# A hybrid decoder trunk on one core: the pre-norm applied in the transposition by a diagonal matrix, the first tiles in a fixed order, keys and values post-processed for all tiles at once

## The chip, the cores and the metric

The kernel runs on one core of a Trainium2 chip. The core has five engines with queues of their own: TensorE (PE in the profile, its weight loads PEld), VectorE (DVE), ScalarE (ACT), GpSimd (POOL) and SyncE (SP), which issues nearly all DMAs. The metric is the device time of one execution in microseconds, lower is better; a figure for a kernel is the median of several runs.

## The reference

Two layers (DEPTH = 2) over 512 tokens of width 1024, all in float32. Each layer normalises its input, projects it once, runs two kinds of heads side by side, projects back and adds the normalised result.

```python
def hybrid_layer(x, w_in, w_out, g_pre, g_post, lb, g_head, sinks):
    h = rms_norm(x, g_pre)                    # x * rsqrt(mean(x^2) + 1e-6) * g
    proj = h @ w_in                           # 1024 -> 6400
    q_h, f_h, i_h, z_h, q_a, k_a, v_a, z_a = split(proj)
    o_h = hgrn2(q_h, f_h, i_h, lb)            # gated linear recurrence, 8 heads of 128
    o_h = rms_norm(o_h, g_head) * silu(z_h)
    q_a, k_a = rotary(q_a), rotary(k_a)       # 16 query heads, 2 key and 2 value heads of 64
    o_a = sliding_window_attention(q_a, k_a, v_a, sinks) * silu(z_a)
    y = concat(o_h, o_a) @ w_out              # 2048 -> 1024
    return x + rms_norm(y, g_post)
```

## The kernel before

The tokens are four tiles of 128 (`NT`), the model width eight blocks of 128 (`KT`). A float32 product is made of three products of halves: each operand is split into a high part `hi`, rounded to the fast float32 type of TensorE (ScalarE, a copy), and the rest `lo` (VectorE, a subtraction), and `mm3` (L174 to L177) adds lo x hi, hi x lo and hi x hi into one PSUM tile.

**Weights** come as pieces of 128 x 512 numbers in one fixed list (`plan`, L108 to L133). `w_load` puts a piece into one of three raw buffers, `w_conv` (L156 to L172) splits it: L169 on ScalarE, L170 on VectorE, or on GpSimd for every second piece of the key/value slab and of the query slab QA. Four pieces hold the key and value columns of a layer (256 columns, two blocks of 128 rows a piece).

**Projections** are units (`Unit`): one PSUM tile of 128 x 512 (128 x 256 for keys and values), eight blocks k long (four for the output projection). `step` issues one block (three products) of a unit and alternates between two units, the next one being started when the first is half done. After each step it runs what has been put off: `later(steps, key, fn)` queues a function that is emitted some steps on, `ensure` forces it where a unit needs its result. Each layer begins with four key/value units, one per token tile (`ORDER`, L122), with the tile of h as stationary operand and the weights moving; then come two slabs of queries with the weights stationary, and so on. The last slab of a layer is the output part "h1", eight units in order of token tiles, each evacuated by L719 and followed by `final` (L732 to L756): post-norm, residual, store of the new x, and for the next layer the pre-norm of that tile.

**Pre-norm** (`pre_norm`, L296 to L318). Per tile: two squares with a sum on ScalarE (L302), the factor r by one small VectorE operation and a power on GpSimd (`rstd2`, L280 and L282), then for each half of the width x * r * gain on VectorE (L306), four transposes on TensorE (L311), and the split of the transposed block into `hhi` (L267, ScalarE) and `hlo` (L268, VectorE). At the start this is emitted at once for all four tiles; at the layer boundary the transposes and the split are put off by 18 steps (`DEFER`). The gain is loaded from memory broadcast over the partitions (`load_g`).

**Keys and values** (`kv_evac`, L329 to L366). Per token tile the unit is copied from PSUM (L339), rotated by six VectorE operations of 64 columns (L346 to L351), doubled (L352), the values split (L365, L366), and 16 steps later the keys transposed (L358) and split. Attention reads them after both query slabs.

**The start** (L792 to L851) loads x tile 0, the identity, the broadcast gain, then key/value pieces and the other x tiles in turn, runs six warm-up products, the four pre-norms, and prepares masks, tables and the lower bounds of the gate.

The order on each engine is a static schedule: the program is recorded, and a scheduler orders each engine's instructions by the program's order and its own model of readiness. Only instructions marked with `pin` keep the program's order; `tc.high_priority` moves some ahead. DMA queues and engines work their instructions in order, waiting where an operand is not there.

Of the kernel before, what the change touches and what calls it, by code (L numbers as in the profile page):

```python
# [10 lines left out]
F32 = mybir.dt.float32  # L11
# [21 lines left out]
RAW_BUFS = 3  # L33
# [6 lines left out]
FB = 8  # L40
# [25 lines left out]
def hybrid_kernel(ctx: ExitStack, tc: tile.TileContext, x, wkv, win, wout, g_pre, g_post, lbp, ghead, sinks,  # L66
# [78 lines left out]
    state = {"raw": 0, "conv": 0}  # L145
# [10 lines left out]
    def w_conv(n):  # L156
        w_load(n)
        while state["conv"] < min(n, len(pieces)):
            i = state["conv"]
            if i in kv_pieces and kv_pieces[i] not in kv_room:  # L160
                return
# [7 lines left out]
            nc.scalar.copy(hi, v)  # L169
            (nc.gpsimd if i in on_pool and i % 2 else nc.vector).tensor_tensor(lo, v, hi.bitcast(F32), op=ALU.subtract)  # L170
# [3 lines left out]
    def mm3(o, sta, mov, start, stop):  # L174
        nc.tensor.matmul(o, lhsT=sta[1], rhs=mov[0], start=start, stop=False)  # L175
        nc.tensor.matmul(o, lhsT=sta[0], rhs=mov[1], start=False, stop=False)  # L176
        nc.tensor.matmul(o, lhsT=sta[0], rhs=mov[0], start=False, stop=stop)  # L177
# [19 lines left out]
    class Unit:  # L197
        def __init__(self, key, ks, sta, mov, evac, needs, ncol):
            self.key, self.ks, self.sta, self.mov, self.evac, self.needs, self.ncol = key, list(ks), sta, mov, evac, needs, ncol
            self.i = 0  # L200

# [9 lines left out]
    def step():  # L211
        if not active or (len(active) == 1 and units and 2 * (len(active[0].ks) - active[0].i) <= len(active[0].ks)):
# [10 lines left out]
        k = u.ks[u.i]  # L223
        mm3(u.o, u.sta(k, u.w), u.mov(k, u.w), u.i == 0, u.i == len(u.ks) - 1)
# [71 lines left out]
    def pre_norm(tt, xt, g, hT, key, defer=0):  # L296

        ss = sm.tile([P, 2], F32, tag="ss", name="ss")
        xn2 = big.tile([P, 2, 512], F32, tag="q", name="xn", bufs=QB)
        for c in range(2):  # L300
            junk = tmp("u")
            nc.scalar.activation(junk, xt[c], AF.Square, scale=1.0 / 32.0, accum_out=ss[:, c:c + 1])  # L302
        r = rstd2(ss)
        for c in range(2):
            xn = xn2[:, c]
            nc.vector.scalar_tensor_tensor(xn, xt[c], r, g[c], op0=ALU.mult, op1=ALU.mult)  # L306

            def rest(c=c, xn=xn):
                o = sc()
                for j in range(4):  # L310
                    pin(nc.tensor.transpose(o[:, j * P:(j + 1) * P], xn[:, j * P:(j + 1) * P], ident))  # L311
# [599 lines left out]
```

## Time and profile before

| | |
|---|---|
| median of 3 runs | 956.77 us (952.09 to 960.68) |
| profiled execution | 954.91 us, its span 953.2 us |
| mean granted TensorE clock | 0.989 |
| TensorE busy | 918.9 us, 96% |
| VectorE busy | 681.9 us, 72% |
| ScalarE busy | 475.2 us, 50% |
| GpSimd busy | 267.3 us, 28% |

Times in the profile are microseconds from the first instruction; a mean duration in a group is in nanoseconds. A row of the timeline gives start, duration, engine, line of the kernel, operation, what is written and read, the number of instructions, and in brackets the idle time before it with what ended it. A group gives shapes, count, busy time, mean duration, idle time ahead of it and its cause. Matmuls are pipelined: the distance from start to start, not the duration shown, is what a product costs. A clock of 1.00 is full speed of TensorE.

### The profile page before, as it was taken

How to read it: one execution, taken by the hardware profiler on the slowest of the kernel's cores; microseconds unless marked ns; L12 is line 12 of the kernel's file. 1: busy time of each engine (PE TensorE's matmuls, PEld its weight loads, DVE VectorE, ACT ScalarE, POOL GpSimd, SP SyncE). 2: the span in 40 equal slices, each digit the busy share in tenths (PEclk: the TensorE clock that was granted, in tenths of full speed). 3: DMA queues.
4: the chain of work that ended last, by engine and by line, in shares of the span. 5: the costliest groups of instructions: out<-in, count | busy, mean ns of one | idle time of the engine just before them, and what ended most of it. 6: DMA issues, size and time to landing. Idle time of an engine off the chain costs nothing.

```text
span 953.2 us, 19110 instructions
## 1 busy us (share of the span) xinstructions
PE 918.9 (96%) x7228; PEld 754.8 (79%) x7228; DVE 681.9 (72%) x1382; ACT 475.2 (50%) x1135; POOL 267.3 (28%) x282
## 2 busy tenths in 40 slices
PE   7999998999999999999969989989999999999996
PEld 5887887778878788788868878877788887887885
DVE  5866878796766685865795678778867578749546
ACT  5524766836464462434553257677363645414242
POOL 2232454422231221311331235434322213113102
PEclk8999999999999999999999999999999999999999
DMA  6456622232222332323443665122222233413313
GB/s 219 145 177 175 186 72 79 66 90 68 78 79 81 87 112 89 112 69 118 132 158 123 178 180 150 54 70 67 90 67 69 88 89 84 129 55 103 89 46 132
DMA packets 56716, 101.34 MB, mean 106 GB/s; under 512 B 6448, under 2 KB 8880, under 8 KB 56624
## 3 DMA queue, kind: packets, MB, share of 16 engines
q1 hardware_dynamic: 56624, 100.12, 35.5%
q8 instruction: 57, 0.93, 0.4%
q14 instruction: 35, 0.29, 0.1%
HBM read 87.52 MB, written 12.58 MB: 105 GB/s over the span
## 4 chain that ended last, share of the span: by engine, by line
PE 77%; DVE 9%; ACT 6%; issue 4%; POOL 2%; DMA 1%; SPq 0%; DVEq 0%; POOLq 0%; ACTq 0%
PE pj L175 22%; PE pj L177 21%; PE pj L176 21%; DVE wlo L170 3%; ACT s L442 2%; PE sc L583 2%; PE sc L428 2%; PE ac L652 1%; PE ac L481 1%; PE ac L640 1%; ACT whi L169 1%; PE ac L655 1%; DVE xn L306 1%; PE sc L455 1%; PE sc L700 1%
## 5 line engine op out<-in xcount | busy, mean ns | idle before, releaser
L169 ACT CAST whi<-raw 128x512 fp32r<-128x512 f32 x256 | 158.2, 620 | 193.5 <-PE pj L177 154.3
L170 DVE TENSOR_TENSOR wlo<-raw,whi 128x512 fp32r<-128x512 f32 x248 | 185.4, 753 | 63.0 <-ACT whi L169 61.0
L175 PE MATMUL pj<-hhi,wlo 128*128 128x512 f32 x512 | 206.4, 403 | 0.0
L177 PE MATMUL pj<-hhi,whi 128*128 128x512 f32 x512 | 200.8, 392 | 0.0
L176 PE MATMUL pj<-hlo,whi 128*128 128x512 f32 x512 | 200.2, 391 | 0.0
L177 PEld LDWEIGHTS pj<-hhi,whi 128*128 128x128 f32 x512 | 96.6, 189 | 21.0
L175 PEld LDWEIGHTS pj<-hhi,wlo 128*128 128x128 f32 x512 | 96.6, 189 | 18.7
L176 PEld LDWEIGHTS pj<-hlo,whi 128*128 128x128 f32 x512 | 96.8, 189 | 18.2
L175 PE MATMUL pj<-whi,hlo 128*128 128x512 f32 x256 | 103.2, 405 | 3.6 <-ACT whi L169 3.6
L175 PE MATMUL pj<-whi,ops 128*128 128x512 f32 x256 | 103.8, 406 | 0.0
L176 PE MATMUL pj<-wlo,hhi 128*128 128x512 f32 x256 | 100.4, 392 | 0.0
L177 PE MATMUL pj<-whi,ops 128*128 128x512 f32 x256 | 100.1, 391 | 0.0
L177 PE MATMUL pj<-whi,hhi 128*128 128x512 f32 x256 | 100.1, 391 | 0.0
L176 PE MATMUL pj<-wlo,ops 128*128 128x512 f32 x256 | 99.7, 390 | 0.0
L601 POOL TENSOR_TENSOR k<-k,tot 128x256 f32<-128x256 f32 x80 | 65.0, 832 | 109.9 <-PE sc L583 64.0
L175 PEld LDWEIGHTS pj<-whi,hlo 128*128 128x128 f32 x256 | 48.2, 188 | 12.6 <-ACT whi L169 4.5
L449 POOL TENSOR_TENSOR s<-s,sums 128x512 f32<-128x512 f32 x32 | 34.9, 1091 | 81.9 <-DVE sums L447 34.3
L177 PEld LDWEIGHTS pj<-whi,ops 128*128 128x128 f32 x256 | 48.0, 188 | 10.7
L600 DVE TENSOR_TENSOR q<-q,tot 128x256 f32<-128x256 f32 x80 | 46.9, 614 | 13.1 <-PE sc L583 8.6
L177 PEld LDWEIGHTS pj<-whi,hhi 128*128 128x128 f32 x256 | 48.1, 188 | 10.1
L175 PEld LDWEIGHTS pj<-whi,ops 128*128 128x128 f32 x256 | 48.1, 188 | 9.3
L176 PEld LDWEIGHTS pj<-wlo,ops 128*128 128x128 f32 x256 | 48.2, 188 | 9.0
(172 smaller groups left out, 1587.0 us busy)
## 6 DMA issues: line engine op xcount, KB each, us to landing
raw<-in_win_dram SPq DMA_DIRECT2D x192, 256.0 KB, 2.7
raw<-in_wout_dram SPq DMA_DIRECT2D x64, 256.0 KB, 2.7
stack<-rot SPq DMA_DIRECT2D x16, 512.0 KB, 3.9
qs<-stack SPq DMA_DIRECT2D x32, 256.0 KB, 4.4
a<-in_x_dram SPq DMA_DIRECT2D x12, 256.0 KB, 3.1
raw<-in_wkv_dram SPq DMA_DIRECT2D x8, 256.0 KB, 4.0
x_mid<-a SPq DMA_DIRECT2D x8, 256.0 KB, 2.1
a<-x_mid SPq DMA_DIRECT2D x8, 256.0 KB, 3.2
```

Source lines behind the costliest of these rows:

```text
L169: nc.scalar.copy(hi, v)
L170: (nc.gpsimd if i in on_pool and i % 2 else nc.vector).tensor_tensor(lo, v, hi.bitcast(F32), op=ALU.subtract)
L175: nc.tensor.matmul(o, lhsT=sta[1], rhs=mov[0], start=start, stop=False)
L176: nc.tensor.matmul(o, lhsT=sta[0], rhs=mov[1], start=False, stop=False)
L177: nc.tensor.matmul(o, lhsT=sta[0], rhs=mov[0], start=False, stop=stop)
L306: nc.vector.scalar_tensor_tensor(xn, xt[c], r, g[c], op0=ALU.mult, op1=ALU.mult)
L428: pin(nc.tensor.matmul(S[:, h * 256:(h + 1) * 256], lhsT=q[:, 2 * hp_ + h, t_], rhs=kst[v][p][:, (n - 1) * P:(n + 1) * P], start=(h == 0 a ...
L442: nc.scalar.activation(pt[:, h * P:(h + 1) * P], cur[h], AF.Exp, bias=negm[:, h:h + 1], scale=SCALE, accum_out=sums[:, h:h + 1])
L449: nc.gpsimd.tensor_tensor(pv, pv, sums.unsqueeze(2).broadcast_to([P, 4, P]), op=ALU.mult)
L583: pin(nc.tensor.matmul(L[32 * b:32 * b + 32, c:c + 16], lhsT=k[:, o_:o_ + 32], rhs=qv[:, blk:blk + qu, 1, :], start=True, stop=True, tile_ ...
L600: nc.vector.tensor_tensor(qv[:, :, 1, :], qv[:, :, 1, :], tv[:, :, 0].unsqueeze(2).broadcast_to([P, nb, hh]), op=ALU.mult)
L601: nc.gpsimd.tensor_tensor(kv_[:, :, 0, :], kv_[:, :, 0, :], tv[:, :, 1].unsqueeze(2).broadcast_to([P, nb, hh]), op=ALU.mult)
```

## The change

Pre-norm: x times gain is computed ahead of r (`weigh`), and instead of a transpose with the identity TensorE multiplies that block with a diagonal matrix that holds r (`diag`, `turn`), so that scaling and transposition are one float32 product. The gain sits in PSUM. The square writes into the place of `hlo`, which is overwritten later. At the start one square covers a whole tile, EPS is added on GpSimd, and nearly all of the work of the first two tiles and of the key/value pieces is pinned in an order written out by hand; tiles 1 to 3 follow as deferred functions. The gain row of layer 0 is spread over the partitions by a product with ones; it and the identity are loaded from ScalarE's queue.

Key/value units issue their 24 products in another order (hi x hi of all eight k, then hi x lo, then lo x hi) and are not interleaved with other units. Rotation, split and transposition of keys and values are done once for all four tiles. A limit keeps query weights from being converted before the last tile of h is turned (none at the start, two at the boundary), query pieces after that are converted in program order, and one piece of layer 1 moves from GpSimd to VectorE. There are four raw buffers. Tables, masks and lower bounds are loaded and computed after four query steps.

```diff
-RAW_BUFS = 3
+RAW_BUFS = 4
...
+    for l in range(1, DEPTH):
+        on_pool.discard(slab_first["in", l, QA][0] + 1)
+    in_turn = set(range(KT // 2, KT))
+    for l in range(1, DEPTH):
+        in_turn.update(slab_first["in", l, QA][0] + j for j in range(2, KT))
...
+            if state["limit"] is not None and i >= state["limit"]:
+                return
...
-            nc.scalar.copy(hi, v)
-            (nc.gpsimd if i in on_pool and i % 2 else nc.vector).tensor_tensor(lo, v, hi.bitcast(F32), op=ALU.subtract)
+            keep = pin if i in in_turn else lambda ins: ins
+            keep(nc.scalar.copy(hi, v))
+            keep((nc.gpsimd if i in on_pool and i % 2 else nc.vector).tensor_tensor(lo, v, hi.bitcast(F32), op=ALU.subtract))
...
+    EACH = [(1, 0), (0, 1), (0, 0)]
+    def products(ks, fresh):
+        if not fresh:
+            return [(k, i, j) for k in ks for i, j in EACH]
+        return [(k, i, j) for i, j in ((0, 0), (0, 1), (1, 0)) for k in ks]
...
-        if not active or (len(active) == 1 and units and 2 * (len(active[0].ks) - active[0].i) <= len(active[0].ks)):
+        if not active or (len(active) == 1 and units and not active[0].fresh and not units[0].fresh
+                          and 2 * (len(active[0].ks) - active[0].i) <= len(active[0].ks)):
...
+    class Norm:
...
+        def rstd(self):
+            if self.whole is None:
+                self.r = rstd2(self.ss)
+                return
+            t = sm.tile([P, 1], F32, tag="s1", name="s1")
+            pin(nc.gpsimd.tensor_scalar(t, self.ss[:, 0:1], EPS, None, op0=ALU.add))
+            self.r = sm.tile([P, 1], F32, tag="r1", name="r1")
+            pin(nc.gpsimd.tensor_tensor(self.r, t, mhalf[:, 0:1], op=ALU.pow))
+        def weigh(self, c):
+            return nc.vector.tensor_tensor(self.xg[:, c], self.xt[c], self.g[c], op=ALU.mult)
+        def diag(self):
+            return nc.vector.tensor_scalar(self.dg[:, self.tt], ident, self.r, None, op0=ALU.mult)
+        def turn(self, c):
+            self.o[c] = o = sc()
+            for j in range(4):
+                pin(nc.tensor.matmul(o[:, j * P:(j + 1) * P], lhsT=self.xg[:, c, j * P:(j + 1) * P], rhs=self.dg[:, self.tt],
+                                     start=True, stop=True))
+            self.o[c] = o.rearrange("p (k t) -> p k t", k=4)
...
+    def pre_norm(tt, xt, g, hT, key, dg, defer):
+        m = Norm(tt, xt, g, hT, dg)
+        m.square()
+        m.weigh(0)
+        m.weigh(1)
+        m.rstd()
+        m.diag()
+        later(defer, None, lambda: m.rest(0))
+        later(defer, key, lambda: m.rest(1))
...
+            nc.scalar.copy(rkv[0][:, tt], o)
+            if tt == NT - 1:
+                later(12 if l == 0 else 8, None, kv_rotate)
+                later(24 if l == 0 else 16, ("k", l, 0), kv_store)
...
+                        hT2["gpre"] = [ac() for _ in range(2)]
+                        for c, t in enumerate(load_g(g_pre[l + 1])):
+                            nc.scalar.copy(hT2["gpre"][c], t)
+                        hT2["dg"] = diagonals()
+                        state["limit"] = slab_first["in", l + 1, QA][0] + 2
...
+    for c in range(2):
+        nc.scalar.dma_start(grow[c], g_pre[0:1, c * 512:(c + 1) * 512])
+    nc.scalar.dma_start(ident, ident_c)
     xts = [x_tile(0)]
...
+    w_load(2)
     for tt in range(1, NT):
         xts.append(x_tile(tt))
+        w_load(4)
...
+    warm = pj()
+    nc.tensor.matmul(warm, lhsT=ones[:, 0:P], rhs=ones, start=True, stop=True)
+    gpre = [ac() for _ in range(2)]
+    for c in range(2):
+        nc.tensor.matmul(gpre[c], lhsT=ones[0:1, 0:P], rhs=grow[c], start=True, stop=True)
...
+    m, n = head[0], head[1]
+    pin(m.square())
+    pin(m.weigh(0))
+    m.rstd()
+    pin(m.diag())
+    pin(m.weigh(1))
+    kv_high(0, nc.scalar.copy)(V)
+    kv_high(1, nc.scalar.copy)(G)
+    m.turn(0)
+    pin(m.high(0))
+    m.turn(1)
+    pin(m.high(1))
+    low2 = kv_high(2, nc.scalar.copy)
+    pin(n.square())
+    pin(n.weigh(0))
+    low3 = kv_high(3, nc.vector.tensor_copy)
+    low3(G)
+    pin(m.low(0))
+    low2(V)
+    n.rstd()
+    pin(n.weigh(1))
+    pin(n.diag())
+    pin(m.low(1))
...
+    def head_rest(tt):
+        if tt + 1 < NT:
+            front(head[tt + 1])
+        for c in range(2):
+            head[tt].turn(c)
+            pin(head[tt].high(c))
+            pin(head[tt].low(c))
+        if tt == NT - 1:
+            state["limit"] = None
+    for tt in range(1, NT):
+        later(8 * tt - 2, ("h", 0, tt), lambda tt=tt: head_rest(tt))
...
+    later(8 * NT + 4, None, constants)
```

More of the change, by code (lines that the diff above doesn't have):

```diff
@@ L200, in __init__ @@
             self.i = 0
+            self.fresh = key[0] == "kv"
+            self.list = products(self.ks, self.fresh)
     units, active, turn, slab_steps, slab_done = deque(), [], [0], {}, {}
@@ L222, in step @@
         turn[0] += 1
-        k = u.ks[u.i]
-        mm3(u.o, u.sta(k, u.w), u.mov(k, u.w), u.i == 0, u.i == len(u.ks) - 1)
+        for n in range(3 * u.i, 3 * u.i + 3):
+            k, i, j = u.list[n]
+            nc.tensor.matmul(u.o, lhsT=u.sta(k, u.w)[i], rhs=u.mov(k, u.w)[j], start=(n == 0), stop=(n == len(u.list) - 1))
         u.i += 1
@@ L369, in layer, with rkv_rot, kv_store @@
+        kks = []
+        def rkv_rot():
+            kks.append(tmp("b", n=2).rearrange("p a (n v d) -> p (a n) v d", n=2, v=2))
+            return kks[0]
+        def kv_store():
+            for v in range(2):
+                kt = sc()
+                for tt in range(NT):
+                    pin(nc.tensor.transpose(kt[:, tt * P:(tt + 1) * P], kks[0][:, tt, v, :], ident))
+                split_psum(kst[v][0], kst[v][1], kt)
+            emitted.update(("k", l, tt) for tt in range(NT))
         qs = {}
@@ L792, in hybrid_kernel @@
+    mhalf = const.tile([P, 4], F32, name="mhalf")
+    grow = [tmp("z0")[0:1, :] for _ in range(2)]
+    for c in range(2):
+        nc.scalar.dma_start(grow[c], g_pre[0:1, c * 512:(c + 1) * 512])
+    nc.scalar.dma_start(ident, ident_c)
     xts = [x_tile(0)]
-    ident = const_tile(ident_c, [P, P], F32, "ident")
-    mhalf = const.tile([P, 4], F32, name="mhalf")
+    ones = tmp("u")
+    nc.vector.memset(ones, 1.0)
     nc.vector.memset(mhalf, -0.5)
-    gpre = load_g(g_pre[0])
-    w_load(1)
+    w_load(2)
@@ new lines, in hybrid_kernel, with front, kv_high @@
+    gpre = [ac() for _ in range(2)]
+    for c in range(2):
+        nc.tensor.matmul(gpre[c], lhsT=ones[0:1, 0:P], rhs=grow[c], start=True, stop=True)
+    hT[0] = new_hT()
+    dg = diagonals()
+    head = [Norm(tt, [xts[tt][:, 0], xts[tt][:, 1]], gpre, hT[0], dg, xts[tt]) for tt in range(NT)]
+    def front(m):
+        pin(m.square())
[3 more added lines that the diff above has]
+        pin(m.diag())
+    def kv_high(i, eng):
+        raw = raws.pop(i)
+        conv[i] = tuple(big.tile([P, 512], F32R, tag="v", name="wkv", bufs=8) for _ in range(2))
+        pin(eng(conv[i][0], raw))
+        return lambda eng: pin(eng(conv[i][1], raw, conv[i][0].bitcast(F32), op=ALU.subtract))
@@ new lines, in hybrid_kernel @@
+    V, G = nc.vector.tensor_tensor, nc.gpsimd.tensor_tensor
+    m, n = head[0], head[1]
+    pin(m.square())
+    pin(m.weigh(0))
+    m.rstd()
+    pin(m.diag())
+    pin(m.weigh(1))
+    kv_high(0, nc.scalar.copy)(V)
[12 more added lines that the diff above has]
+    n.rstd()
```

192 lines of the change are left out of this document (90 added, 102 removed).

## The prediction

> **What bounds the kernel now.** I read the page first, then the table of what TensorE waits for, then the two stretches that table points to, by stage windows and by the timeline.
>
> ```profile
> span 953.2 us, 19110 instructions
> PE 918.9 (96%) x7228; PEld 754.8 (79%) x7228; DVE 681.9 (72%) x1382; ACT 475.2 (50%) x1135; POOL 267.3 (28%) x282
> PE pj L175 <- DVE hlo L268: 7.3, 3, 5.7
> PE sc L311 <- DVE xn L306: 4.1, 2, 2.5
> ```
>
> TensorE is busy for 96% of the span, so a change that is not about its work can only win the places where it stands still. The waits (engine, line, what it waited for: us in total, times, longest) name where: L311 and L175 behind L306 and L268 are the pre-norm, its normalisation, its transposition and the low half of the transposed tile. They lie at the start and at the boundary between the two layers. The stage windows of the two stretches (busy time of each engine with its instruction count, then granted clock, DMA share, GB/s):
>
> ```profile
> core 0: us, PE busy (x) PEld busy (x) DVE busy (x) ACT busy (x) POOL busy (x), PEclk, DMA share, GB/s
> 0.00:10.90 10.90, 6.89 (x13) 2.84 (x13) 2.14 (x7) 4.64 (x10) 1.72 (x7) 1.00 0.76 242
> 10.90:15.00 4.10, 2.49 (x12) 1.85 (x13) 2.19 (x5) 2.97 (x9) 1.79 (x2) 0.55 0.96 306
> 15.00:18.30 3.30, 3.30 (x18) 3.30 (x17) 2.93 (x6) 2.34 (x6) 0.54 (x1) 0.52 0.02 2
> 18.30:34.34 16.04, 14.81 (x114) 13.85 (x113) 15.30 (x45) 9.54 (x25) 5.76 (x5) 1.00 0.53 166
> 477.20:482.90 5.70, 0.01 (x1) 0.01 (x1) 5.26 (x9) 1.96 (x6) 2.09 (x2) 0.95 0.46 148
> 482.90:486.20 3.30, 3.30 (x18) 3.30 (x18) 3.18 (x5) 2.29 (x8) 1.80 (x2) 0.56 0.64 220
> 486.20:502.94 16.74, 15.10 (x116) 14.18 (x115) 15.26 (x43) 9.15 (x27) 3.65 (x4) 1.00 0.45 142
> ```
>
> In the first 10.9 us TensorE does only warm-up products; then come slivers at half clock (0.55, 0.52). At the boundary it stands 5.7 us with VectorE busy for 5.26 of them, and then runs 3.3 us at 0.56. These two stretches, 34.3 us and 25.7 us long, are where the time can change.
>
> **The head, step by step.** The rows of the timeline (start, duration) that set its order:
>
> ```profile
> 4.43 0.63 ACT L302 ACTIVATE u<-a 128x512 f32<-128x512 f32 x1 [0.35 <-DMA a<-in_x_dram]
> 5.43 0.54 POOL L282 TENSOR_TENSOR r<-s,mhalf 128x1 f32<-128x1 f32 x1 [3.66 <-DVE s L280]
> 10.09 1.41 DVE L306 SCALAR_TENSOR_TENSOR xn<-a,r,b 128x512 f32<-128x512 f32 x2
> 14.13 1.28 DVE L268 TENSOR_TENSOR hlo<-sc,hhi 128x512 fp32r<-128x512 f32 x2
> 15.04 0.56 PE L175 MATMUL pj<-wkv,hlo 128*128 128x256 f32 x1
> 27.83 0.28 PE L176 MATMUL pj<-wkv,hhi 128*128 128x256 f32 x1
> 27.95 0.28 PE L177 MATMUL pj<-wkv,hhi 128*128 128x256 f32 x1
> 31.20 0.40 PE L175 MATMUL pj<-hhi,wlo 128*128 128x512 f32 x1
> 31.43 0.40 PE L176 MATMUL pj<-hlo,whi 128*128 128x512 f32 x1
> 33.29 0.40 PE L175 MATMUL pj<-hhi,wlo 128*128 128x512 f32 x1
> 34.34 0.27 PE L358 MATMUL sc<-ident,s 128*128 128x128 f32 x1
> 233.90 0.89 PE ac L652 x8
> 493.86 1.03 PE L311 MATMUL sc<-ident,xn 128*128 128x128 f32 x8
> L169 ACT CAST whi<-raw 128x512 fp32r<-128x512 f32 x256 | 158.2, 620 | 193.5 <-PE pj L177 154.3
> 475.68 1.05 ACT L267 CAST hhi<-sc 128x512 fp32r<-128x512 f32 x2
> L268 DVE TENSOR_TENSOR hlo<-sc,hhi 128x512 fp32r<-128x512 f32 x16 | 10.7, 682 | 0.7 <-ACT hhi L267 0.7
> L272 POOL TENSOR_SCALAR hr<-hss 128x4 f32<-128x4 f32 x16 | 3.8, 235 | 107.4 <-DVE hss L660 107.1
> ```
>
> The factor of tile 0 is there at 5.97 (5.43 + 0.54), yet its normalised tile is begun only at 10.09, behind a key/value conversion, and the first projection starts at 15.04, because it begins with the low half of the tile. Key/value products follow each other by 0.12 us (27.83 to 27.95), 512-column ones by 0.23. All 96 key/value products are out by 34.34; nine query products (three triples, 31.20 to 33.29, 9 x 0.23 = 2.07) and two key transposes (about 0.11 each) lie among them. Without these the head ends at 34.34 - 2.07 - 0.22 = 32.05.
>
> *Price of the diagonal.* A transposition becomes a real fp32 product of x times gain with diag(r). Eight transposes take 1.03 from the first start to the last end with 0.27 for one, so 0.76/7 = 0.109 apart, 0.44 for four. L652 is the nearest row of an fp32 128x128 product, in the recurrence: in the chain of waits four products stand as eight instructions in 0.89. So four turned blocks cost 0.89 instead of 0.44; 16 groups (two per tile, eight tiles) put 16 x 0.45 = 7.2 us more on TensorE. From both sides: 0 if the product ran as the transposes do, 7.2 by L652. I take L652, whose operands have the same type and size. This is hidden only where TensorE would stand still.
>
> *New chain.* x tile 0 is complete at 4.43 as before (it is issued first in both). One square over both halves, at most 2 x 0.63, ends at 5.7. From the square's end to the start of the power 0.37 pass now (5.06 to 5.43); with the addition of EPS moved to GpSimd (0.24) I allow 0.5, then 0.54: r at 6.8. Scaling the 128x128 identity by r has a quarter of the 512 columns for which L268 takes 0.68: between 0.17 and 0.68, I take 0.3, since a fixed part remains: 7.1. The weighting x * gain no longer waits for r. Its gain comes by two products of a 2 KB row with ones, 0.89 each by L652 (512 columns), 1.8 at half clock: had the row landed only with x at 4.43, the second would be ready at 8.0 and turn 1 some 0.6 late; as it is tiny and on a queue of its own I take no delay. The broadcast loads of the gain, 512 KB, are gone from the start; three small loads are issued by ScalarE instead of SP, which costs nothing under ScalarE's wait for x until 4.43. Turn 0 is over at 8.0, its high half (L267, 0.53 each) at 8.6; turn 1 and its high half at 9.5. The first key/value products now use high halves alone, for all eight k, so TensorE starts at 9 instead of 15.04. They also need all four key/value pieces: x tiles 0 and 1 and four pieces are 8 x 256 KB = 2.1 MB, at the 242 GB/s of the first window 8.7 us; no delay beyond the fixed order; a fourth raw buffer lets the first query weights follow them. On ScalarE that order is high 0, high 1, cast of piece 2 (0.62), square of tile 1: 9.5 + 0.62 + 1.26 = 11.4; with GpSimd and the diagonal 12.7. From there TensorE has per tile 24 x 0.12 = 2.9 of products and 1.78 of turning: tile 1's turns to 14.5, the last six products of tile 0 to 15.2, tiles 1 and 2 with the turns of 2 and 3 to 24.5, tile 3 to 27.4. VectorE needs 4 x 0.68 + 0.3 = 3.0 per tile, less than 4.7, so TensorE sets the pace.
>
> *Clock.* If the first stretch runs at half clock, as 15.00:18.30 does (0.52 for 3.3 us), that adds up to half of 3.3 us, 1.7: 29.1. I take 28.3, the middle. Gain of the head: 32.05 - 28.3 = 3.8, between 2.9 and 4.7. The Trainium skill (TensorE: Matmul & The Clock Gate, PE-mode transpose) says that transposes do not count as activity for the clock; by that rule the turned blocks, being real products, would lift the clock earlier, and the head would end at 27.4. The 0.55 in 10.90:15.00, where transposes are all TensorE does, agrees, but an idle stretch lies there too.
>
> **The boundary.**
>
> ```profile
> 467.35 1.30 POOL L747 TENSOR_TENSOR y<-y,b 128x512 f32<-128x512 f32 x1
> 467.38 2.47 DVE L306 SCALAR_TENSOR_TENSOR xn<-a,r,b 128x512 f32<-128x512 f32 x2
> 482.16 0.68 DVE L268 TENSOR_TENSOR hlo<-sc,hhi 128x512 fp32r<-128x512 f32 x1
> 482.89 0.58 PE L175 MATMUL pj<-wkv,hlo 128*128 128x256 f32 x1 [5.71 <-DVE hlo L268]
> 499.81 0.39 PE L175 MATMUL pj<-hhi,wlo 128*128 128x512 f32 x1
> 501.90 0.40 PE L175 MATMUL pj<-hhi,wlo 128*128 128x512 f32 x1
> 502.82 0.28 PE L177 MATMUL pj<-wkv,hhi 128*128 128x256 f32 x1
> L719 DVE TENSOR_TENSOR y<-pj,y 128x512 f32<-128x512 f32 x48 | 32.8, 684 | 3.5 <-PE pj L177 3.1
> L753 DVE SCALAR_TENSOR_TENSOR a<-y,r,a 128x512 f32<-128x512 f32 x8 | 8.0, 1001 | 3.9 <-POOL r L282 3.7
> ```
>
> The high half of tile 0 is there at 476.73; the low half comes at 482.84, because VectorE has a queue. In the new order the 16 products that need only the high half come first, 16 x 0.12 = 1.9 us, and VectorE is relieved: conversions of query weights beyond two are held back until the last tile is turned, and the weighting reads one operand from PSUM. L268, which reads PSUM too, takes 0.682. Two of L306, reading SBUF alone, take 1.41 undisturbed (10.09) and 2.47 here, while GpSimd's L747 runs; two weightings and a diagonal take 1.36 + 0.3. The gain goes to PSUM by two copies on ScalarE, 2 x 0.62, early in the output products, where ScalarE is far from busy (1.96 of 5.7): nothing.
>
> The small key and value operations per tile leave the boundary for one batch 8 steps after it (12 at the head), eight VectorE operations of 256 columns and two of 512; its transposes come 8 to 12 steps later. By L268's 0.68 for 512 columns that is 8 x 0.34 + 1.4 = 4.1 to 6.8 us of VectorE, and no DMA. It runs beside query products, which leave VectorE one operation in eight steps; attention reads the keys only after both query slabs, 64 steps. I cost it at nothing under that cover, at up to 6.8 without it.
>
> TensorE's own work from 477.2: 0.9 more for tile 0's turns, 3 x 1.78 for the others, 96 x 0.12 = 11.5: 494.9 if nothing waits. Before, the same point is 502.94 - 2.07 (three triples, 499.81 to 501.90) - 0.22 = 500.65. At most 5.8 is to be won; at worst 3.6 are lost, the eight dearer groups, if no idle time closes. VectorE still has about 7.1 us per tile (two of L719, two weightings, two low halves and the product with the post gain, seven at 0.68; L753 twice at 1.0; the diagonal) against 24 x 0.23 = 5.5 of TensorE per output tile (eight steps of three), so it trails by 1.6 per tile, 6.4 after four, when the last output product is out. The key/value stage then gives it 3 x 4.7 = 14 us before tile 3's low half is wanted, 6.4 + 7.1 = 13.5. That is tight, so I let 1.2 us of waiting stand: gain 4.6, to 496.1.
>
> **Sum.** The profiled execution took 954.91 with a span of 953.2. 3.8 + 4.6 = 8.4: 946.5 on that scale. The median of the runs shown, 956.77, is 1.9 above the profiled one; 956.77 - 8.4 = 948.4. The runs lie 8.6 apart.
>
> **Rivals.**
>
> *The diagonal is locked out by GpSimd* (chance 0.17). Row for it:
>
> ```profile
> 25.18 1.29 POOL L170 TENSOR_TENSOR wlo<-raw,whi 128x512 fp32r<-128x512 f32 x1 [2.89 <-ACT whi L169]
> 25.27 1.25 DVE L824 TENSOR_SCALAR nsnk<-snk 128x32 f32<-128x32 f32 x1
> ```
>
> A 32-column scaling took 1.25 and ended with GpSimd's operation. The new diagonal is a scaling of the same kind, now on the path from r to TensorE, and GpSimd starts L747 as soon as r is out (467.35, right as L306 began). Three tiles of the boundary can meet it, 3 x 1.25 = 3.7 lost: gain 4.7, 952.1. Against it: a short diagonal may slip in first, and deferral by 18 steps gives slack to all but the last tile, which has no L747 behind it. The Trainium skill (SBUF — State Buffer, two separate sides) states this as an exclusive lock of the port pair shared by the two engines, taken by single-source VectorE operations in SBUF; by that rule 952.1 would come out, and the rows agree.
>
> *TensorE pays and the idle time stays* (0.10). 7.2 us of dearer turning lie on an engine busy for 96%; if VectorE still delivers tiles at its old pace (its 5.26 of 5.7 busy speaks for it), the span grows by them: 963.9. It decides once less than 7.2 of the idle and half-clock time is recovered. At the head 9 instead of 15.04 speaks against.
>
> *All gaps close* (0.15). The head from 7.1 with 8 x 0.89 + 11.5 = 18.6 unbroken, 25.7, and the boundary at 494.9: 6.3 + 5.8 = 12.1, 944.7.
>
> *Constants come late* (0.08). Their six loads move to behind weight loads that wait for buffers on SP, and VectorE's copies of them, in fixed order, hold query evictions queued behind them. With one buffer wait of eight query steps (8 x 3 x 0.23 = 5.5) the gain falls to 2.9: 953.9.
>
> **Chances.** Forecast 0.50, its own range 944 to 953 (half the spread of runs either way); the rivals as given. Low end 941, below all gaps closed less run spread; high end 958, which leaves out the second rival and tails. About 1%, 9.6 us, is what a measurement here can tell from no change. Faster by more than that, below 947.2: most of the third rival and some half of the forecast, 0.41. Slower by more, above 966.3: the second rival's upper part and unseen orders, 0.08. Within: 0.51.
>
> **What would show it.** The first key/value product near 9 to 11 and the last near 28; no 5.7 us wait at 477 and no half clock after; turned blocks in pairs of records, 0.89 for four; the diagonal at 0.3 or, by the first rival, at 1.3. A wait of TensorE for a low half of over 3 us at the boundary, or for a diagonal, would make it wrong, as would new waits between 30 and 45.

## The result and the profile after

The changed kernel takes 948.61 us (median of 6 runs, 947.22 to 949.39), the kernel before in the same comparison 958.03 (6 runs, 952.09 to 960.68). The ratio is 0.9907, 95% interval 0.9884 to 0.9931: 0.9% faster, against a forecast of 948.4. The profiled execution took 947.43 us with a span of 945.3, 7.9 less than the span before. The first lines of the page after, and TensorE's waits (engine, line, what it waited for: us in total, times, longest):

```profile
span 945.3 us, 19154 instructions
PE 918.9 (97%) x7286; PEld 757.0 (80%) x7286; DVE 679.6 (72%) x1328; ACT 471.9 (50%) x1098; POOL 267.9 (28%) x285
```

```profile
PE sc L498 <- ACT s L512: 11.8, 11, 2.6
PE sc L352 <- DVE hlo L361: 1.4, 1, 1.4
PE sc L352 <- DVE z L347: 1.2, 2, 1.1
PE pj L240 <- ACT wkv L900: 0.6, 1, 0.6
```

TensorE's busy time is the same as before, 918.9 us, so the span is shorter by just the time in which it no longer stands. That equality is a sum of two changes: the turned blocks are busy for 7.2 us more than the transposes were (18.1 against 10.9 us for their lines), and less work runs at half clock, as is shown below. The waits of 7.3 and 4.1 us behind the pre-norm are gone; 1.4 (the low half at the boundary) and 1.2 (the diagonal at the start) are left. The 11.8 us behind L512 lie in the attention, which the change does not touch; the trace before counts 5.9 us there and 3.6 behind the high half of a weight (L169), at the same places of the body (1.41 us at 87.92 and 2.22 at 556.56 before, 2.02 at 82.92 and 2.16 at 547.56 after). The stage windows after (busy time of each engine with its instruction count, then granted clock, DMA share, GB/s):

```profile
core 0: us, PE busy (x) PEld busy (x) DVE busy (x) ACT busy (x) POOL busy (x), PEclk, DMA share, GB/s
0.00:8.36 8.36, 5.79 (x7) 1.67 (x7) 1.53 (x5) 3.46 (x5) 2.24 (x9) 1.00 0.73 246
8.36:12.29 3.93, 3.93 (x18) 3.93 (x19) 3.25 (x5) 0.70 (x2) 2.34 (x2) 1.00 1.05 373
12.29:15.68 3.39, 2.60 (x20) 2.20 (x19) 1.63 (x4) 3.08 (x6) 1.03 (x3) 1.00 0.79 210
15.68:31.62 15.94, 15.94 (x130) 15.70 (x131) 10.28 (x16) 8.70 (x19) 4.45 (x6) 1.00 0.28 83
474.85:493.76 18.91, 17.41 (x145) 17.03 (x144) 13.29 (x24) 10.33 (x25) 6.02 (x6) 1.00 0.35 119
```

From 15.68 on TensorE does not stop in the head, and at the boundary it is busy for 17.41 of 18.91 us, where it stood 5.7 us at one stroke before. Rows of the timeline after (start, duration):

```profile
4.56 1.28 ACT L327 ACT_TABLE_LOAD   x1 [4.56 <-DMA a<-in_x_dram]
5.85 1.06 ACT L327 ACTIVATE hlo<-a 128x1024 fp32r<-128x1024 f32 x1
8.02 0.29 DVE L347 TENSOR_SCALAR z<-ident,r 128x128 f32<-128x128 f32 x1 [1.71 <-POOL r L341]
8.36 3.78 PE L352 MATMUL sc<-z,xg 128*128 128x128 f32 x16 [1.07 <-DVE z L347]
11.79 0.94 PE L240 MATMUL pj<-wkv,hhi 128*128 128x256 f32 x4
13.18 1.06 ACT L327 ACTIVATE hlo<-a 128x1024 fp32r<-128x1024 f32 x1
15.68 0.49 PE L352 MATMUL sc<-z,xg 128*128 128x128 f32 x2 [0.18 <-DVE z L347]
20.21 1.95 PE L352 MATMUL sc<-z,xg 128*128 128x128 f32 x16
30.25 0.40 PE L240 MATMUL pj<-hhi,wlo 128*128 128x512 f32 x1
483.44 1.16 PE L352 MATMUL sc<-z,xg 128*128 128x128 f32 x8 [1.36 <-DVE hlo L361]
493.76 0.40 PE L240 MATMUL pj<-hhi,wlo 128*128 128x512 f32 x1
```

The first query product, with which the key/value stage is over, starts at 30.25 in layer 0 and at 493.76 in layer 1; by the same count these points stood at 32.05 and 500.65. So the span's 7.9 us fall into three parts. The **head** is 1.8 shorter. The **boundary** is 3.6 shorter: from the end of the output products to the query products it took 500.65 - 477.20 = 23.45, and now takes 493.76 - 474.85 = 18.91 plus 0.92. The 0.92 is what the turned blocks of tile 0 take more than its transposes did (1.95 against 1.03); both lie ahead of the stretch that is counted. The remaining **2.5 us** are in the body of the two layers, where the change edits little; the next part shows what they are.

### Where 2.5 us came from without an edit

In the body before, half clock appears twice, at 158 and at 629 us, right after an attention wait. That wait, 2.55 to 2.58 us, is there in both kernels. Windows of the kernel before and then of the one after, cut to 3.41 us:

```profile
154.70:158.11 3.41, 1.38 (x7) 0.80 (x5) 3.38 (x6) 1.27 (x4) 1.86 (x2) 1.00 0.63 169
158.11:161.52 3.41, 2.89 (x11) 2.69 (x12) 2.78 (x8) 1.26 (x9) 1.00 (x2) 0.50 0.18 63
...
478.97:482.38 3.41, 0.00 (x0) 0.00 (x0) 3.14 (x4) 0.78 (x3) 1.46 (x2) 1.00 0.65 214
482.38:485.79 3.41, 2.90 (x13) 2.90 (x14) 3.29 (x5) 2.62 (x7) 1.80 (x2) 0.50 0.74 246
```

```profile
152.24:155.65 3.41, 2.58 (x12) 1.78 (x10) 3.41 (x9) 1.10 (x2) 0.67 (x1) 1.00 0.37 98
155.65:159.07 3.42, 1.70 (x11) 1.61 (x12) 3.34 (x7) 1.60 (x9) 1.86 (x2) 1.00 0.43 132
159.07:162.48 3.41, 3.41 (x18) 2.81 (x18) 2.23 (x8) 2.21 (x9) 1.04 (x1) 1.00 0.02 5
```

The cut is not arbitrary. Every half-clock stretch that begins between 20 us and 935 us in the 14 traces of this case lasts 3.41 us, which costs up to half of it, 1.71, and within one trace their starts lie whole multiples of 3.4133 us apart, to 0.01: in the kernel before 158.11, 482.38 and 629.15 are 95 and 43 steps apart. So the clock changes step by step on a grid that runs through, and what goes with a change is how much of one step TensorE stood. In the first fence it stood 2.03 of 3.41 us and the next step ran at half clock; in the second the same wait falls across a step's edge (0.83 and 1.72), and nothing follows. Of these 32 half-clock steps, 30 follow a step with at least 1.97 us of standing (58%; gaps over 0.3 us counted), one follows 1.88 and one 1.54; no step with more than 1.89 kept its clock. The Trainium skill (TensorE: Matmul & The Clock Gate, What's actually happening) describes a free-running window of 3413 ns, and the traces agree. The Trainium skill's rule of thumb on the same page (HAM oscillation, "no PE-idle gaps >~3.4µs") is too mild here: gaps of 2.01 us were enough where one window held them.

Two such steps (158.11 and 629.15) are 3.4 us that the profiled run before lost and the one after did not, from waits that both have. Against them the body took 0.9 us longer otherwise, which leaves the 2.5. The grid's position against the kernel differs from trace to trace, so in a single run this part is a matter of luck. All runs together: with "lost" for span x (1 - mean granted clock), an upper bound for what half clock cost, and "rest" for span less that, each the mean over the runs,

| kernel | median us | ratio to before, same comparison | lost | rest |
|---|---|---|---|---|
| before (in three comparisons: 13, 27, 24 runs) | 958.2, 956.7, 956.6 | | 12.4, 11.9, 12.2 | 943.7, 943.1, 943.3 |
| after | 948.61 | 0.9907 (0.9884 to 0.9931) | 3.2 | 943.2 |
| early table | 947.93 | 0.9895 (0.9880 to 0.9911) | 4.3 | 941.7 |
| more warm-up | 949.01 | 0.9908 (0.9893 to 0.9922) | 6.2 | 940.7 |
| transposes | 944.47 | 0.9860 (0.9844 to 0.9877) | 4.7 | 938.5 |
| old product order | 955.50 | 0.9972 (0.9951 to 0.9993) | 7.1 | 945.8 |
| keys and values per tile, 3 raw buffers | 952.49 | 0.9946 (0.9919 to 0.9972) | 5.7 | 944.6 |
| 3 raw buffers | 952.18 | 0.9945 (0.9924 to 0.9966) | 5.4 | 944.9 |
| no hold | 954.03 | 0.9980 (0.9964 to 0.9997) | 7.0 | 944.8 |
| gain in SBUF | 951.84 | 0.9948 (0.9928 to 0.9968) | 5.9 | 944.3 |
| product order alone | 958.52 | 1.0014 (0.9992 to 1.0037) | 11.6 | 945.3 |
| transposes, table, pinned copy | 951.51 | 0.9939 (0.9919 to 0.9959) | 9.0 | 940.5 |
| the same, more warm-up | 951.18 | 0.9945 (0.9926 to 0.9964) | 10.0 | 939.8 |
| after, table, more warm-up | 951.38 | 0.9920 (0.9886 to 0.9954) | 4.9 | 943.4 |

One run of the product order alone, of 4251 us, is left out of its row. The column "lost" has two faults. The clock record of a trace starts late, at 12.29 in the run after, 4.51 in the one before and 4.59 with more warm-up, and what comes ahead of it counts as full clock. So the 1.83 us that the first turned blocks of the run after take longer than later ones (3.78 against 1.95, in the rows above) stand under "rest" there, while "more warm-up" has its slow head under "lost". And 2.3 us of the run after are a half-clock stretch behind its last product, which costs nothing; every trace has one like it.

Before and after differ by 9.4 us, and nearly all of it stands in the column "lost". As printed, the rest is the same; with the 1.83 moved to "lost" it is about 2 us less than before. So the idle time that the change closes is little more than what its dearer turned blocks cost. About 5 us of lost clock belong to long stops that the change removed (3.4 between 11.3 and 18.2 in the head, of which the slow turned blocks give 1.8 back, and 1.7 at 482). The other 4 or so are steps after waits that are still there. Whether they are luck is open: all six runs after lost 1.9 to 3.8, the runs before 7.6 to 16.3, and no run moved the grid alone. Differences of one or two such steps between kernels of this table should not be read as the effect of an edit.

### The profile page after: what moved, and what is told of

Its sections match the earlier page's. It is cut to its first block, busy times and chain, and to the rows that moved or that the text cites. A ratio compares the mean times of both kernels' runs of the same rounds, so it can differ in the third digit from the quotient of the medians.

```text
span 945.3 us, 19154 instructions
## 1 busy us (share of the span) xinstructions
PE 918.9 (97%) x7286; PEld 757.0 (80%) x7286; DVE 679.6 (72%) x1328; ACT 471.9 (50%) x1098; POOL 267.9 (28%) x285
## 4 chain that ended last, share of the span: by engine, by line
PE 77%; DVE 10%; ACT 5%; issue 4%; POOL 2%; DMA 1%; SPq 0%; DVEq 0%; POOLq 0%; ACTq 0%
PE pj L240 64%; DVE wlo L178 3%; PE sc L653 2%; ACT s L512 2%; PE ac L722 2%; PE sc L498 1%; PE ac L710 1%; PE ac L551 1%; PE ac L725 1%; PE sc L352 1%; DVE oa L557 1%; ACT whi L177 1%; PE sc L770 1%; DVE mx L503 1%; DVE sc L502 1%
## 5 line engine op out<-in xcount | busy, mean ns | idle before, releaser
L178 DVE TENSOR_TENSOR wlo<-raw,whi 128x512 fp32r<-128x512 f32 x249 | 189.5, 767 | 56.3 <-ACT whi L177 54.4
L240 PE MATMUL pj<-whi,ops 128*128 128x512 f32 x512 | 173.6, 398 | 0.0
L240 PEld LDWEIGHTS pj<-hlo,whi 128*128 128x128 f32 x512 | 96.3, 188 | 18.2
L512 ACT ACTIVATE s<-sc,negm 128x128 f32<-128x128 f32 x128 | 45.6, 369 | 25.0 <-DVE negm L506 22.9
L240 PEld LDWEIGHTS pj<-wlo,hhi 128*128 128x128 f32 x256 | 48.3, 189 | 7.7
```

The lines of the kernel that those rows point to most:

```text
L178: keep((nc.gpsimd if i in on_pool and i % 2 else nc.vector).tensor_tensor(lo, v, hi.bitcast(F32), op=ALU.subtract))
L240: nc.tensor.matmul(u.o, lhsT=u.sta(k, u.w)[i], rhs=u.mov(k, u.w)[j], start=(n == 0), stop=(n == len(u.list) - 1))
L512: nc.scalar.activation(pt[:, h * P:(h + 1) * P], cur[h], AF.Exp, bias=negm[:, h:h + 1], scale=SCALE, accum_out=sums[:, h:h + 1])
```

## The experiments

Line numbers in the edits are left out; each is an edit of the changed kernel unless it says otherwise.

### The diagonal taken back

r is computed ahead of the weighting, x times r times the gain is formed at once, and the block is transposed with the identity.

```diff
-            return nc.vector.tensor_tensor(self.xg[:, c], self.xt[c], self.g[c], op=ALU.mult)
+            return nc.vector.scalar_tensor_tensor(self.xg[:, c], self.xt[c], self.r, self.g[c], op0=ALU.mult, op1=ALU.mult)
...
-                pin(nc.tensor.matmul(o[:, j * P:(j + 1) * P], lhsT=self.xg[:, c, j * P:(j + 1) * P], rhs=self.dg[:, self.tt],
-                                     start=True, stop=True))
+                pin(nc.tensor.transpose(o[:, j * P:(j + 1) * P], self.xg[:, c, j * P:(j + 1) * P], ident))
```

> The changed kernel without the diagonal matrix: x times factor times gain on VectorE after the factor is known, then transposes; all else as changed. Theory (TensorE sets the pace from tile 1 on, and a turned group of four costs 0.45 us more than four transposes): six groups of the head and seven of the boundary come off its path, 13 x 0.45 = 5.9 us, against 0.4 us of longer chain at the first tile: 943. Rival (the chain from factor to low half sets the pace, VectorE is the bound): 948 to 950, with new waits of TensorE for the normalised tile.

944.47 us, 4.1 faster than with the diagonal, and the intervals of the two ratios do not touch. The timeline of this kernel:

```profile
17.58 1.59 PE L240 MATMUL pj<-wkv,hhi 128*128 128x256 f32 x11 [1.11 <-ACT hhi L356]
19.86 1.03 PE L352 MATMUL sc<-ident,xg 128*128 128x128 f32 x8
28.07 0.40 PE L240 MATMUL pj<-hhi,wlo 128*128 128x512 f32 x1
```

Eight transposes take 1.03 where the eight turned blocks of a tile take 1.95, and the head ends 2.2 us earlier (28.07 against 30.25), though r now stands ahead of the weighting and a new wait of 1.11 came in. From there to the first query product of layer 1 it is another 2.1 us shorter (489.49 - 28.07 against 493.76 - 30.25), with no half clock in either trace, so the two stages give the 4.1 without help from the clock. The forecast, 5.9 less 0.4, was somewhat too high. The kernel is better without the part of the change that gives it its name; its "rest" falls by 4.7.

### The first turned blocks: table and warm-up

The first row of ScalarE's timeline above shows a table load of 1.28 us behind x; before, it was over at 2.06, under the wait for x. Two edits, a tiny square ahead of x that brings the table early, and three warm-up products in place of one:

```diff
+    nul = sm.tile([P, 1], F32, tag="nul", name="nul", bufs=1)
+    pin(nc.scalar.activation(nul, mhalf[:, 0:1], AF.Square))
     w_load(2)
```

> The changed kernel with one tiny square on ScalarE at the start, so that the function table is loaded while x is on its way (in the changed kernel the load runs from 4.56 to 5.84, after x has landed). Theory (the chain from x tile 0 to its factor sets the start): the first factor comes at 6.7 instead of 7.98, the first turned block at 7.1 instead of 8.36, the head ends 1.3 us earlier, 947.3 in all. Rival (key/value pieces or the gain are next late): less than 0.5 us, 948.3 or more.

```diff
-    nc.tensor.matmul(warm, lhsT=ones[:, 0:P], rhs=ones, start=True, stop=True)
+    for _ in range(3):
+        nc.tensor.matmul(warm, lhsT=ones[:, 0:P], rhs=ones, start=True, stop=True)
```

> The changed kernel with three warm-up products of 128 rows instead of one. In the changed kernel the first 16 records of turned blocks take 3.78 us, later groups 1.95. Theory (TensorE is at half clock there, because the two products that spread the gain use one row and do not lift the clock): with two more full products the first 16 records take 1.95 to 2.2, the head ends 1.5 to 2 us earlier, 946.8. Rival (the granted clock is shown as 1.00 there, so the turned blocks are slow for another reason, or the clock drops again in the idle stretch ahead): no change, 948.6.

With the early table the first turned block starts at 7.51 in place of 8.36 and the head ends at 29.38 (0.87 less); x landed later in this run, so the square started at 5.01. The median, 947.93, is 0.7 lower, which these runs cannot tell from none. This run also lost a half-clock step in the body, behind the wait of 2.02 us at 82 that the kernel after passed unharmed:

```profile
81.54:84.95 3.41, 1.40 (x9) 0.93 (x8) 2.87 (x12) 2.08 (x12) 0.29 (x1) 1.00 0.00 0
84.95:88.36 3.41, 3.41 (x13) 2.77 (x12) 2.26 (x9) 1.97 (x9) 1.19 (x2) 0.50 0.00 0
```

The warm-up did nothing for the time (949.01). Its timeline, and two windows on its grid; the last two lines are windows of the run of transposes with table, pinned copy and more warm-up, whose edits follow below:

```profile
5.79 1.98 PE L886 MATMUL ac<-z,u 1*128 1x512 f32 x4
8.74 3.78 PE L352 MATMUL sc<-z,xg 128*128 128x128 f32 x16 [0.97 <-DVE z L347]
```

```profile
4.60:8.01 3.41, 3.17 (x7) 0.85 (x5) 0.69 (x1) 3.05 (x5) 0.45 (x2) 1.00 1.01 328
8.01:11.43 3.42, 2.69 (x12) 2.69 (x13) 2.90 (x5) 0.98 (x2) 1.73 (x3) 0.50 1.04 378
...
4.89:8.31 3.42, 3.42 (x8) 0.95 (x8) 0.75 (x1) 2.00 (x4) 1.50 (x3) 1.00 1.04 366
8.31:11.72 3.41, 3.18 (x14) 2.52 (x14) 2.65 (x5) 2.00 (x4) 1.85 (x2) 0.50 1.07 382
```

Three full products did lift the clock here: the two products that spread the gain take 1.98, where they take 3.78 after one. But these read one row of 128. In 4.60:8.01 TensorE shows 3.17 us of work and still the next step is at half clock. In 4.89:8.31 of the other run it does not stand at all, and the next step is at half clock too. These are the only two traces whose clock record covers such products, so they seem to count as standing still; no run was made for this alone.

To keep the clock, full products were then put ahead of each one-row product, with the diagonal and without it. The second pair of runs also has the early table, and pins the copy of the key/value product (L396), because the wait of 1.11 above came from a square that ran ahead of a high half on ScalarE.

```diff
-            nc.scalar.copy(rkv[0][:, tt], o)
+            (pin if l == 0 else lambda ins: ins)(nc.scalar.copy(rkv[0][:, tt], o))
...
+        for _ in range(2 - c):
+            pin(nc.tensor.matmul(warm, lhsT=ones[:, 0:P], rhs=ones, start=True, stop=True))
         pin(nc.tensor.matmul(gpre[c], lhsT=ones[0:1, 0:P], rhs=grow[c], start=True, stop=True))
```

> Edit: the changed kernel, diagonal kept, with the tiny early square and the same three warm-up products between the one-row gain products. Theory (half-speed turning of tile 0 is the clock, lost over the one-row products): the first 16 records of turning take 1.95 as later groups do instead of 3.78, the first key/value product starts 1.8 to 2.6 earlier than 11.79, and the kernel is near 945.5. Rival (idle time or something else than the one-row products sets that speed): the 16 records take 3.78 again and only the early table's 0.7 is gained, 947.9.

> Edit: the changed kernel with plain transposes (x times r times gain by one VectorE operation once r is there, no diagonal), a tiny square on ScalarE ahead of x so that its table is loaded early, and the copy of the key/value product out of PSUM in layer 0 kept in the program's order on ScalarE. Theory (the diagonal's dearer products cost some 4 us net, the table load stands on the path, and the 1.11 us wait of the run with transposes alone came from a square that ran ahead on ScalarE): the three add up, 944.5 - 0.7 - 1.0 = 942.8, head end near 26.3 to 27 where the transposes alone had 28.07, no wait of TensorE for hhi in layer 0's key/value stage. Rival (the head is bound by VectorE and by the weight pieces once the transposes are cheap): no change against transposes alone, 944.5, head end within 0.3 of 28.07, with waits for hlo or wkv in the place of those removed.

> Edit: the same, and three full 128-row warm-up products stand ahead of and between the two one-row gain products. Theory (TensorE runs the first transposes at half speed because one-row products do not count as work for the clock): a full product right ahead of each one-row product keeps the clock, the first transposes take their full-speed time, and the kernel is 0.5 to 1.5 us faster than without the warm-ups, near 941.8. Rival (the idle time between the gain products and the first transposes drops the clock whatever stands before): no gain over the same kernel without them, first transposes as slow as there.

All three miss. With the diagonal (951.38) the added products themselves ran at half clock, 1.9 each, and pushed the first turned block to 11.22; in the run without the diagonal the same products had full clock from 4.89, so where the grid lay is the likely cause. Without the diagonal the warm-up made no difference (951.51 and 951.18). The transposes with early table and pinned copy do end the head at 25.85, 2.2 earlier than the transposes alone, as the theory said, and the kernel is yet 7 us slower than those. Timeline and grid of the run without warm-up:

```profile
25.85 0.40 PE L240 MATMUL pj<-hhi,wlo 128*128 128x512 f32 x1
33.53 0.62 ACT L177 CAST whi<-raw 128x512 fp32r<-128x512 f32 x1 [1.35 <-DVE wlo L178]
34.05 0.36 ACT L396 COPY rkv<-pj 128x256 f32<-128x256 f32 x1
34.47 0.50 PE L240 MATMUL pj<-hhi,wlo 128*128 128x512 f32 x1 [2.99 <-ACT rkv L396]
```

```profile
31.54:34.95 3.41, 0.48 (x2) 0.43 (x3) 2.62 (x3) 2.05 (x5) 1.27 (x1) 1.00 0.73 238
34.95:38.36 3.41, 3.41 (x10) 2.63 (x9) 1.29 (x2) 0.00 (x0) 0.00 (x0) 0.50 0.67 226
```

The pin put the last tile's copy behind casts of query weights, which wait for their loads (2.06, 0.96 and 0.82 us between 25 and 31) and once for VectorE (the 1.35 in the rows). TensorE needs the place that this copy frees and stands 2.99 us, and a half-clock step follows: 4.7 together, more than the 2.2 won. In the trace of the transposes alone this copy goes ahead at 28.27. Over all runs 4.3 of the 7 us stand under "lost" (9.0 against 4.7) and 2.0 under "rest". In the profiled run the step behind the copy is 1.7 of it; the others follow waits of the body that both kernels have.

### The order of the key/value products and what it leans on

The three products of a block together again; and, in the kernel before, the order by halves as the only edit:

```diff
-            self.list = products(self.ks, self.fresh)
+            self.list = products(self.ks, False)
```

> The changed kernel with the three products of each block of keys and values together again, low half of the tile first; units still not interleaved. Theory (the order by halves takes the low half off the path): TensorE waits again for low halves, at the head until about 16.3 instead of 11.8 for the second half of tile 0, and at the boundary from 474.9 to about 477 and again for tile 3; 4 to 7 us more, 953 to 956. Rival (VectorE's relief alone closes the gaps): within 1 us, 949.

> Edit: the kernel before, with one part of the change alone: key/value units issue their products by halves (high by high for all eight blocks, then high by low, low by high) and are not interleaved with others. Theory (the waits for the low half are what the change removes, and the order by itself removes most of them): 952 to 954 against 957, the 5.7 us wait at the boundary shrinks to 3 to 4, since the high half of tile 0 is there at 476.7 but VectorE's queue still holds the second tiles' normalisation. Rival (the order is worth something only together with a relieved VectorE): within 1 us of the kernel before, the wait moves from the first product to the ninth to seventeenth.

Without the order the kernel is 6 to 7 us slower (by the ratios and by the medians); with the order alone, no faster than before. Waits of the first and then of the second:

```profile
PE pj L240 <- DVE hlo L361: 5.6, 3, 2.2
```

```profile
PE sc L317 <- DVE hlo L274: 4.2, 1, 4.2
PE sc L317 <- DVE xn L312: 3.7, 3, 1.9
PE pj L230 <- DVE hlo L274: 1.0, 1, 1.0
```

In the first the key/value products wait for low halves three times. In the second they hardly do (1.0), but the stop has only moved: the transposes of the next tile now wait for the low half of the tile before (4.2 at once), and as before for their own normalised tile (3.7, where it was 4.1). That VectorE's queue is as long as it was explains both. So the order pays only together with the rest of the change: alone it gives nothing, the rest without it 2.7 us, both together 9.4. Two edits undo parts of VectorE's relief, the hold on query conversions at the boundary (with their fixed order in layer 1) and the gain in PSUM:

```diff
-        in_turn.update(slab_first["in", l, QA][0] + j for j in range(2, KT))
...
-                        state["limit"] = slab_first["in", l + 1, QA][0] + 2
```

> The changed kernel without the hold on query-weight conversions at the boundary (no limit, and no fixed order for them in layer 1; the start keeps both). Theory (the hold keeps VectorE and GpSimd free for the last tiles): six conversions, 0.7 to 1.4 us on VectorE and 1.3 on GpSimd each, go in between, and TensorE waits 2 to 4 us more between 475 and 494: 951 to 953. Rival (the order by halves covers them): within 1 us, 948.6.

```diff
-                        hT2["gpre"] = [ac() for _ in range(2)]
-                        for c, t in enumerate(load_g(g_pre[l + 1])):
-                            nc.scalar.copy(hT2["gpre"][c], t)
+                        hT2["gpre"] = load_g(g_pre[l + 1])
```

> The changed kernel with the gain of layer 1 left in SBUF instead of copied to PSUM. Theory (VectorE with two operands in SBUF is held up while GpSimd works): the weighting at the boundary takes 1.7 us instead of 0.68 where GpSimd runs at its start, about one in two, 4 us more of VectorE, 1 to 2 us on the path: 950. Rival (the weighting no longer waits for the factor and so seldom meets GpSimd): within 0.5 us.

Without the hold 954.03, and the low half is waited for again. Waits of that kernel:

```profile
PE sc L350 <- DVE hlo L359: 3.9, 2, 2.4
```

With the gain in SBUF 951.84, and its boundary has two waits, 1.6 (for a high half) and 1.5 (for a low half), in place of one of 1.4. By the ratios the hold is worth 7 us, 1.6 of it in "rest", and the gain in PSUM 4 us, 1.1 of it in "rest"; what of the lost clock beside it is chance is open.

### Keys and values per tile, and the fourth raw buffer

The batch frees the room for the fourth raw buffer, so the two were parted: three buffers with the batch, and three buffers with the per-tile operations of the kernel before (its rotation, split and transposes put back, with the early loads of their tables).

```diff
-RAW_BUFS = 4
+RAW_BUFS = 3
```

> The changed kernel with three raw buffers. Theory (the fourth buffer moves no wait of TensorE): 948.6, within 1 us, though the fourth key/value piece of the start is loaded a buffer later. Rival (the fourth buffer is what removed TensorE's waits for high halves of weights, 3.6 us in the kernel before): those waits return, 951 to 952.

> The changed kernel with keys and values rotated, split and transposed tile by tile as before (with three raw buffers, since the space for the fourth goes to the small tile of the rotation; to be set against the run with three raw buffers alone; the two rotation tables are loaded ahead of the first unit). Theory (VectorE is nearly full at the boundary, 13.5 of 14 us, so the small operations, about 2.7 us per tile, come on the path): 3 to 5 us more than with three raw buffers alone, with waits of TensorE for low halves or diagonals in both stretches. Rival (they fit in between): within 1 us of it.

952.18 and 952.49: with three buffers the batch makes no difference that these runs show, where 3 to 5 us had been expected of it. With three buffers the fourth key/value piece comes late (0.95 us of waiting at 15.1, a half-clock step after it), and the head ends at 33.15 in place of 30.25. The trace with three buffers counts 3.8 us of waits for high halves of weights again, as the rival said, but the waits behind L512 fall from 11.8 to 5.9 at once: the places are the same (1.62 us at 89.00, 2.21 at 553.28), and only the releaser named is another. So the rival's time came (951 to 952 expected), but not its mechanism. The ratio's interval, 0.9924 to 0.9966, just overlaps that of the changed kernel, and with the same three buffers the per-tile kernel's head ended at 31.09 without such a step, so what the buffer is worth, between 0.8 and 3.6 us, stays open.

## Why the prediction was right, and where it was not

**The total** came out (948.4 forecast, 948.61 measured), but not as the sum had it: 8.4 were forecast as 3.8 at the head and 4.6 at the boundary. In the profiled runs 7.9 came, as 1.8, 3.6 and 2.5 from the body, where two half-clock steps fell away and for which the sum had no term. The medians of the comparison lie 9.4 apart. The right total is partly luck.

**The head** is the term that was mis-sized, in two steps of the new chain: it ended at 30.25, outside the 27.4 to 29.1 that were allowed, and gained 1.8 where at least 2.9 were expected. The first diagonal was put at 7.1 and is ready at 8.31: the table load of 1.28 now stands behind the wait for x. In both kernels the first square calls for it; what puts it behind the wait after, where ScalarE issues three loads before it, the runs do not show. The first turned blocks were given 1.78 and at worst half clock, with 28.3 as the middle; the worst case held, 3.78 for the 16 records of the first tile against 1.95 for a later one. Tile 1's turns so begin at 15.68 in place of 12.7, 3.0 late. From there to the query products 14.57 pass, where 27.4 - 12.7 = 14.7 were forecast: the pace of 4.7 per tile was right. The clock column shows 1.00 over those turns because its record starts at 12.29; that they ran at half clock is read from the 3.78, which the run with more warm-up shows under a recorded 0.50. The hope that real products would lift the clock earlier (27.4) was not met, and the rule behind it, that transposes do not count, is not borne out here. Two of the windows shown with the warm-up speak against it: in 8.31:11.72 eight transposes fill 1.70 of the 3.18 us of work and the next step has full clock, while 2.69 us of turned blocks in 8.01:11.43 did not lift it.

**The price of the diagonal** was right: 1.95 for eight blocks from the first start to the last end, against 1.03 for eight transposes, is 0.46 per group of four where 0.45 was taken. That this price is covered where TensorE stood was half right: taking it back gains 4.1 of at most 7.2.

**The boundary** was right in mechanism. One wait of 1.36 us is left where 1.2 were allowed, no half clock follows, and the order by halves with VectorE relieved is what does it: with the order or the hold taken away, waits for a low half came back there (2.15 more, and 1.51 and 2.37 in place of the 1.36), with the gain in SBUF a wait of 1.6 for a high half. The stage took 1.0 more than forecast, most of it TensorE's own work, 19.83 - 1.36 = 18.5 against 17.7 in the ideal.

**Costed at nothing**, the batch of keys and values cost nothing that the runs show, and won nothing either. The fourth raw buffer was mentioned only in passing, and the head's end may depend on it.

**The rivals.** That GpSimd locks the diagonal out did not occur: L347 takes 287 ns on average over its eight. But in none of the eight was a GpSimd operation running when the diagonal began; at 8.02 and 477.23 one began 0.1 us behind it, so the short operation did slip in first, as the prediction hoped. In the run with early table and more warm-up one was running, and the diagonal took 0.67 us and ended 0.1 behind it, a price of 0.38 us instead of the 1.25 of the forecast; the groups of the changed kernel and the timeline of that run:

```profile
L347 DVE TENSOR_SCALAR z<-ident,r 128x128 f32<-128x128 f32 x8 | 2.3, 287 | 4.0 <-POOL r L341 2.9 <-POOL r L298 0.9
```

```profile
7.25 1.27 POOL L904 TENSOR_TENSOR wkv<-raw,wkv 128x512 fp32r<-128x512 f32 x1 [0.45 <-ACT wkv L903]
7.93 0.67 DVE L347 TENSOR_SCALAR z<-ident,r 128x128 f32<-128x128 f32 x1
```

That TensorE pays while the idle time stays: it pays (7.2 us more in the turned blocks), but the idle time went too. All gaps closed: no, 1.1 and 1.4 are left. Constants late: no new wait lies between 30 and 45.

## What to carry to other kernels

When TensorE is busy nearly all the time, an edit that saves a wait by dearer products on TensorE should be tried without the products: here reordering together with a shorter queue on VectorE brought what the stages gained, and plain transposes are 4 us better. Before a few microseconds are put down to an edit, compare the granted clock of all runs, and look at which steps of the clock's grid hold a wait; a wait of about 2 us can cost 1.7 more or nothing. An instruction pinned in order waits with all that is pinned ahead of it, so pinning a short copy behind conversions that wait for loads and buffers moves the stop rather than removing it.

## What was not expected of the hardware

The half-clock steps come on a grid of 3.4133 us within a run, each costing up to 1.71 us, after a step in which TensorE stood for some 55% or more (the counts are above). This was read from the traces of all kernels; no run was made for it alone, and the step at 490.65 in the run of the order alone, with 1.54 us of standing and half clock after it, is not explained. In two runs a step with about 2 us of one-row products was followed by half clock although TensorE showed 3.17 of 3.41 and 3.42 of 3.42 us busy. In one run a step at half clock with 1.70 us of transposes and 3.18 us of work in all was followed by full clock. A table load can stand behind the wait of the operation that calls for it and so add its 1.28 us to the path (4.56 after, 0.78 before); an operation without a wait ahead of it brought it to 2.04.
